# A two-layer encoder trunk on one core: four weight units by landed tile at the start, another SSD output chain, attention scores by row halves

## The chip, the core and the metric

The kernel runs on one core of a Trainium2 chip. A core has TensorE (PE, matrix products into PSUM), VectorE (DVE), ScalarE (ACT), GpSimd (POOL) and SyncE (SP, which here issues nearly all DMAs). PE's weight loads are listed apart as PEld. The metric is the device time of one execution in microseconds (us); the median of three runs before the change is 2410.8 us (2410.72 to 2411.09).

## The reference

512 tokens of 1024 features go through two layers of four steps. RMSNorm gains and residual sums are in every step:

```
h += 0.5 * swiglu(rmsnorm(h))                  # 1024 -> 2 x 2816 -> 1024
h += mixer(rmsnorm(h))                         # layer 0: SSD, layer 1: attention
h += 0.5 * swiglu(rmsnorm(h))
h += sigmoid(rmsnorm(h) @ Wg) * rmsnorm(p @ Wp)
```

The SSD mixer projects to z, x, B, C and dt, convolves, scans in both directions in chunks of 128 tokens, and ends with

```
y = rmsnorm(y * silu(z), norm_g)               # 2048 features
return y @ w_out
```

The attention has 16 heads of 64 features. The tokens form a grid of 8 x 64; queries go in four blocks of 16 columns (128 tokens), each against 32 columns (256 tokens):

```
q = rmsnorm(q, q_norm) * 64 ** -0.5 ;  k = rmsnorm(k, k_norm)
s = einsum(q_blk, k_blk) + bias                # 128 x 256 per head and block
o = einsum(softmax(s), v_blk)
```

## The kernel before

Activations lie with features on the 128 partitions and tokens along the free axis: `h[k]`, k = 0 to 7, are tiles of 128x512. Products are in float32 by three matmuls of a rounded type: a value is split into a high part (an ACT cast or activation, L183, L186) and the rest (a DVE subtraction, L184, L187); `gemm` (L172) multiplies high by high (L177), high weight by low activation (L178) and low weight by high activation (L179). Weights come in units of 128x1024: SP loads one into `wr` (L154, 4 buffers), ACT casts it to `wh` (L162), DVE subtracts to `wl` (L164); three split units are kept ready, so that the split made now is used some gemms later. One unit makes 24 matmuls of 128x512.

Norms are applied late: a gemm runs on gain times h, and its result is multiplied by the factor R. `SumSq` squares on ACT (L207) and adds on POOL (L211), the last addition on DVE. `rsqrt` (L213) spreads the sum by a matmul (L215) and takes Newton steps on 128x512; `begin` and `end` (L221, L231) are the short form: eight small matmuls (L225), Newton steps on 128x4, eight small matmuls (L235), an ACT copy (L238).

PSUM has five banks for gemms (`mm_bank`) and three for the rest (`px_bank`). Tiles come from pools by tag with a fixed number of buffers (`hs` 8, `t2` 7, `sc` 15, `sq` 4, `md` 24, `rt` 3); who takes a buffer waits for its last reader. A scheduler orders the instructions of each engine from the program; an engine then runs its own queue in order and waits where semaphores tell it to.

The places of the change:

- The start (L966 to L1000): the first two units are split by halves as their tiles land, and `first` runs their 48 matmuls by k, two banks in turn. The squares follow, and `ffn` (L273) takes the factor with `norm.factor()` after the second pair of units (f = 1).
- The SSD output: `out_half` (L698) multiplies y's first 1024 features beside the last head group's scan; `pairs_of` (L684) reads y back from `ydram` into `t` tiles (L690). Then eight gemms (d = 0 to 7) multiply the second half. For each d: DVE adds the first half from PSUM and SBUF (L739), POOL multiplies by the factor r2 (L740), DVE adds the residual (L744), and the next norm's split and square follow.
- The attention (L755 on): `project(j)` makes queries and values of head pair j in four pieces, and beside each piece the pairs already projected go on by one step of `attend`. `stack_keys` and `stack_queries` put the high and the low part of one head on the two partition halves, so that one score is two matmuls of 128 rows and 256 columns (L867). `turn` transposes a block's weights (L901), `weigh` multiplies by the values (L910), block by block.

Of the kernel before, what the change touches and what calls it, by code (L numbers as in the profile page):

```python
# [14 lines left out]
P = 128  # L15
# [32 lines left out]
def trunk(ctx, tc, A, out):  # L48
# [98 lines left out]
    todo, raws, ready = plan(), [], []  # L147
# [9 lines left out]
    def split_unit():  # L157
        load_unit()
        if raws:
            raw, n = raws.pop(0)  # L160
            hi = wp.tile([P, 1024], F32R, name=nm("wh"), tag="wh", bufs=3)
            s.copy(out=hi[:, :n], in_=raw[:, :n])  # L162
# [78 lines left out]
    class Norm:  # L241
# [15 lines left out]
        def count(self, k):  # L257
            self.ss.add(h[k], fast=k == KD - 1)
# [14 lines left out]
    def ffn(norm, nxt, between=lambda: None, first=None):  # L273
# [5 lines left out]
        def gate_up(f):  # L279
            pg, pu = mm_bank(), mm_bank()  # L280
# [4 lines left out]
            gemm(pg, unit(), norm.pairs)  # L285
            gemm(pu, unit(), norm.pairs)
# [109 lines left out]
    def ssd(norm, nxt):  # L396
# [288 lines left out]
        def pairs_of(ks, alloc):  # L685
            res = []
            for k in ks:
                if k < 14:
                    yt = t2()
# [3 lines left out]
                pr = alloc()  # L693
# [33 lines left out]
        for d in range(KD):  # L727
# [16 lines left out]
            v.tensor_add(out=h[d].rearrange("p (c r) -> p r c", c=64), in0=old.rearrange(rows, c=64),  # L744
# [4 lines left out]
    def attention(norm, nxt):  # L749
# [6 lines left out]
        def keys(js):  # L756
# [23 lines left out]
            for i in range(4):  # L780
# [4 lines left out]
                kn = hs()  # L785
                v.scalar_tensor_tensor(out=kn, in0=raw[i], scalar=gqk, in1=rb, op0=ALU.mult, op1=ALU.mult)
                kz.append(kn)

        def stack_keys(j):

            res = []
            for a in range(2):
                kk = md(F32R)
                src = kz[j][a * 64:(a + 1) * 64, :]
                own, other = slice(a * 64, (a + 1) * 64), slice((1 - a) * 64, (2 - a) * 64)
                s.copy(out=kk[own, 0, :], in_=src)
                s.copy(out=kk[other, 0, :], in_=src)
                for x in (own, other):
                    v.tensor_sub(out=kk[x, 1, :], in0=src, in1=kk[own, 0, :])
                res.append(kk)  # L800
            return res

        def stack_queries(qb):

            res = []
            for a in range(2):
                qq = bp.tile([P, T], F32R, name=nm("t2"), tag="t2", bufs=7)
                own, other = slice(a * 64, (a + 1) * 64), slice((1 - a) * 64, (2 - a) * 64)
                s.copy(out=qq[own], in_=qb[own])
                v.tensor_sub(out=qq[other], in0=qb[own], in1=qq[own])  # L810
                res.append(qq)
            return res
# [6 lines left out]
        def project(j):  # L819
# [8 lines left out]
            ks = stack_keys(j)  # L828
# [6 lines left out]
            qs = stack_queries(qb)  # L835
# [15 lines left out]
            made[j] = (bias, qs, ks, rq, vt)  # L851
# [4 lines left out]
        def attend(j):  # L856

            bias, qs, ks, rq, vt = made.pop(j)
            st, pT = {}, {}
            vk = None  # L860
            po = None

            def scores(b):
                pscore = px_bank()
                for a in range(2):
                    for x in range(2):
                        te.matmul(out=pscore[:, a * 256:(a + 1) * 256], lhsT=qs[a][:, b * P:(b + 1) * P],  # L867
                                  rhs=ks[a][:, x, KC0[b] * 8:KC0[b] * 8 + 256], start=x == 0, stop=x == 1)
                x = st[b] = sc()
                for a in range(2):  # L870
                    sl = slice(a * 256, (a + 1) * 256)
                    v.scalar_tensor_tensor(out=x[:, sl], in0=pscore[:, sl], scalar=rq[:, 2 * b + a:2 * b + a + 1],
# [13 lines left out]
            def values():  # L886
                vk_ = md()
                for half in range(2):
                    pv = px_bank()
                    for i in range(4):  # L890
                        b, u = 2 * half + i // 2, i % 2
                        k0 = KC0[b] * 8 + u * P
                        te.transpose(out=pv[:, i * P:(i + 1) * P], in_=vt[:, k0:k0 + P], identity=ident)  # L893
                    s.copy(out=vk_[:, half, :], in_=pv)
                return vk_.rearrange("p x (i d) -> p (x i) d", d=P)
# [9 lines left out]
            def weigh(b):  # L905
                y = pT.pop(b)
                for a in range(2):
                    for u in range(2):
                        i = 2 * a + u
                        te.matmul(out=po[a * 64:(a + 1) * 64, b * P:(b + 1) * P],  # L910
                                  lhsT=vk[:, 2 * b + u, a * 64:(a + 1) * 64], rhs=y[:, i * P:(i + 1) * P],
                                  start=u == 0, stop=u == 1)

            for t in range(7):
                if t < 4:
                    scores(t)
                if t == 0:
                    vk = values()
                if 2 <= t < 6:
                    turn(t - 2)  # L920
                if t == 3:
                    po = px_bank()
                if t >= 3:
                    weigh(t - 3)
                if t == 6:
                    op = opr[j] = md(F32R)
                    split(op, po, None)
                yield

# [24 lines left out]
        for d in range(KD):  # L954
# [3 lines left out]
            else:  # L958
# [11 lines left out]
    begun = [(next(todo),) + tuple(wp.tile([P, 1024], dt, name=nm(t), tag=t, bufs=b)  # L970
                                   for t, dt, b in (("wr", F32, 4), ("wh", F32R, 3), ("wl", F32R, 3)))
             for _ in range(2)]
    wcols = (slice(0, 512), slice(512, 1024))
    s.dma_start(out=cst[:, :C_GM], in_=A["cst"][:, :C_GM])
    s.activation(out=warm, in_=ones_d[:, 0:1], func=AF.Silu)
    for k in range(KD):
        sy.dma_start(out=h[k], in_=A["x"][:, k, :])
        if k in (0, 3):
            for src, raw, hi, lo in begun:
                sy.dma_start(out=raw[:, wcols[k // 3]], in_=src[:, wcols[k // 3]])  # L980
    load_unit()
    load_unit()
    sy.dma_start(out=cst[:, C_GM:], in_=A["cst"][:, C_GM:])
    sy.dma_start(out=msk, in_=A["msk"])
    for k in range(KD):
        n.prep(k, False)
        if k in (0, 3):
            for src, raw, hi, lo in begun:
                sl = wcols[k // 3]
                s.copy(out=hi[:, sl], in_=raw[:, sl])  # L990
                last_lo = v.tensor_sub(out=lo[:, sl], in0=raw[:, sl], in1=hi[:, sl])

    def first(pg, pu, pairs):
# [116 lines left out]
```

## Time and profile before

| | |
|---|---|
| median of three runs | 2410.8 us |
| profiled execution | 2410.27 us, span 2408.5 us |
| PE busy, granted clock | 2379.1 us (99%), 0.997 on the mean |
| DVE, ACT, POOL busy | 1441.3, 965.9, 461.7 us (60, 40, 19%) |
| attention stretch | about 1740 to 1960 us |
| SSD output, second half | about 889 to 957 us |

A busy share is a mean over the whole span. Idle time of an engine beside PE costs nothing unless PE waits for it; so the table says that PE is what the time is made of, and the few gaps in PE's own timeline are what other engines cost. A line number may be that of a helper: L187 is the split of any activation.

### The profile page before, as it was taken

The page shows a single profiled execution, that of the slowest core. Times are in us where ns is not written, and L with a number is a line of the kernel's source. Part 1 is how long each engine was busy: PE and PEld are TensorE (multiplying, and loading weights), DVE is VectorE, ACT ScalarE, POOL GpSimd, SP SyncE. Part 2 cuts the span into 40 slices and gives each one's busy share as a digit, 9 for nine tenths or more (in the row PEclk, how much of TensorE's full clock was granted, in tenths as well). Part 3 has the DMA queues.
Part 4 walks back from the last instruction along what each step waited for, and adds up shares of the span by engine and source line. Part 5 has one row for each costly group of instructions (what it writes and reads, how often), then busy time and mean ns, then how long its engine had stood idle before and what let it go on. Part 6 is the DMA issues. An engine that isn't in the chain of part 4 may idle for free.

```text
span 2408.5 us, 29115 instructions
## 1 busy us (share of the span) xinstructions
PE 2379.1 (99%) x11358; PEld 1953.1 (81%) x11358; DVE 1441.3 (60%) x1940; ACT 965.9 (40%) x1557; POOL 461.7 (19%) x387
## 2 busy tenths in 40 slices
PE   8999999999999998999999999999999999999999
PEld 6888888888888786888887888888777878888887
DVE  6544447877777746554447755444579965444456
ACT  4322224655555653332224433222337753222242
POOL 1110101344554544110003111000100011100120
PEclk9999999999999999999999999999999999999999
DMA  4333333544444542333333333333443323333332
GB/s 169 97 96 96 90 121 102 174 135 139 143 140 140 171 141 79 96 96 97 95 103 91 97 96 97 96 96 92 136 142 113 105 70 96 97 97 96 105 92 75
DMA packets 89418, 265.56 MB, mean 110 GB/s; under 512 B 10928, under 2 KB 11824, under 8 KB 89280
## 3 DMA queue, kind: packets, MB, share of 16 engines
q1 hardware_dynamic: 88992, 263.56, 35.5%
q8 instruction: 89, 1.46, 0.2%
q14 instruction: 49, 0.40, 0.1%
q10 hardware_dynamic: 288, 0.14, 0.0%
HBM read 253.40 MB, written 10.26 MB: 109 GB/s over the span
## 4 chain that ended last, share of the span: by engine, by line
PE 57%; DVE 4%; ACT 1%; POOL 1%; issue 0%; DMA 0%; SPq 0%; POOLq 0%; DVEq 0%
PE ps L178 18%; PE ps L177 18%; PE ps L179 18%; PE ps L910 1%; DVE wl L164 1%; PE ps L867 1%; PE ps L901 1%; DVE md L187 0%; DVE md L355 0%; POOL t L740 0%; DVE sc L198 0%; PE ps L773 0%; PE ps L893 0%; DVE sc L197 0%; DVE rt L199 0%
## 5 line engine op out<-in xcount | busy, mean ns | idle before, releaser
L177 PE MATMUL ps<-md,wh 128*128 128x512 f32 x3184 | 1252.2, 393 | 15.2 <-ACT md L186 9.2
L178 PE MATMUL ps<-md,wh 128*128 128x512 f32 x3184 | 1243.0, 390 | 3.3 <-DVE md L187 3.2
L179 PE MATMUL ps<-md,wl 128*128 128x512 f32 x3184 | 1241.8, 390 | 0.6 <-DVE wl L164 0.6
L162 ACT CAST wh<-wr 128x1024 fp32r<-128x1024 f32 (+1 forms) x403 | 416.5, 1034 | 1036.2 <-PE ps L178 655.5
L177 PEld LDWEIGHTS ps<-md,wh 128*128 128x128 f32 x3184 | 599.4, 188 | 147.2 <-ACT md L186 12.8
L178 PEld LDWEIGHTS ps<-md,wh 128*128 128x128 f32 x3184 | 599.5, 188 | 133.8 <-DVE md L187 7.1
L179 PEld LDWEIGHTS ps<-md,wl 128*128 128x128 f32 x3184 | 599.3, 188 | 125.2 <-DVE wl L164 1.1
L164 DVE TENSOR_TENSOR wl<-wr,wh 128x1024 fp32r<-128x1024 f32 (+1 forms) x403 | 579.6, 1439 | 148.4 <-ACT wh L162 119.4
L300 POOL TENSOR_TENSOR t<-t,sc 128x512 f32<-128x512 f32 x88 | 122.5, 1393 | 1017.8 <-ACT wh L162 741.9
L211 POOL TENSOR_TENSOR sq<-sq,sq 128x512 f32<-128x512 f32 x77 | 110.0, 1428 | 599.8 <-ACT sq L207 598.3
L299 DVE TENSOR_TENSOR t<-ps,rt 128x512 f32<-128x512 f32 x88 | 60.8, 691 | 262.0 <-PE ps L179 262.0
L310 DVE SCALAR_TENSOR_TENSOR hs<-ps,hs 128x512 f32<-128x512 f32 x96 | 66.3, 691 | 228.0 <-PE ps L179 228.0
L295 DVE TENSOR_TENSOR t<-ps,rt 128x512 f32<-128x512 f32 x88 | 60.8, 691 | 126.5 <-PE ps L179 126.4
L494 DVE SCALAR_TENSOR_TENSOR t<-ps,ccw,t 128x510 f32<-128x510 f32 (+1 forms) x180 | 134.0, 744 | 3.2 <-ACT t L490 0.3
L547 POOL TENSOR_TENSOR sc<-sc,sc 128x512 f32<-128x512 f32 x64 | 96.2, 1518 | 71.4 <-ACT sc L537 71.3
L183 ACT CAST md<-t 128x512 fp32r<-128x512 f32 x96 | 59.4, 623 | 124.0 <-POOL t L300 122.0
L535 ACT ACTIVATE sc<-hs,md 128x128 f32<-128x128 f32 x256 | 82.4, 397 | 1.7 <-DMA hs<-crow 1.7
L184 DVE TENSOR_TENSOR md<-t,md 128x512 fp32r<-128x512 f32 x96 | 66.8, 700 | 21.5 <-ACT md L183 21.1
L186 ACT ACTIVATE md<-hs,cst 128x512 fp32r<-128x512 f32 x64 | 45.9, 722 | 61.8 <-DVE hs L744 26.1
L187 DVE SCALAR_TENSOR_TENSOR md<-hs,cst,md 128x512 fp32r<-128x512 f32 x64 | 53.3, 843 | 14.6 <-ACT md L186 14.6
L497 ACT ACTIVATE t<-t 128x512 f32<-128x512 f32 x48 | 30.2, 630 | 79.1 <-DVE t L494 78.5
L562 POOL TENSOR_TENSOR md<-md,md 128x256 f32<-128x256 f32 x64 | 44.1, 723 | 80.6 <-ACT md L558 80.6
(155 smaller groups left out, 1362.7 us busy)
## 6 DMA issues: line engine op xcount, KB each, us to landing
wr<-in_w_gu_dram SPq DMA_DIRECT2D x174, 512.0 KB, 3.5
wr<-in_w_in_dram SPq DMA_DIRECT2D x65, 512.0 KB, 3.7
wr<-in_w_dn_dram SPq DMA_DIRECT2D x64, 448.0 KB, 3.3
wr<-in_w_dn_dram SPq DMA_DIRECT2D x32, 512.0 KB, 3.5
hs<-crow SPq DMA_DIRECT2D x64, 256.0 KB, 4.0
wr<-in_w_qkv_dram SPq DMA_DIRECT2D x24, 512.0 KB, 3.5
hs<-vrow SPq DMA_DIRECT2D x64, 128.0 KB, 3.5
wr<-in_w_out_dram SPq DMA_DIRECT2D x16, 512.0 KB, 4.1
```

The source lines that it names most:

```text
L162: s.copy(out=hi[:, :n], in_=raw[:, :n])
L164: v.tensor_sub(out=lo[:, :n], in0=raw[:, :n], in1=hi[:, :n])
L177: te.matmul(out=pt, lhsT=hi[:, sl], rhs=xp[:, 0, cols], start=first and k == 0, stop=False)
L178: te.matmul(out=pt, lhsT=hi[:, sl], rhs=xp[:, 1, cols], start=False, stop=False)
L179: te.matmul(out=pt, lhsT=lo[:, sl], rhs=xp[:, 0, cols], start=False, stop=last and k == n - 1)
L184: v.tensor_sub(out=dst[:, 1, :], in0=src, in1=dst[:, 0, :])
L211: (v if fast else g).tensor_add(out=self.acc, in0=self.acc, in1=q)
L300: g.tensor_mul(out=um, in0=um, in1=sg)
L310: v.scalar_tensor_tensor(out=h[d], in0=pt, scalar=0.5, in1=h[d], op0=ALU.mult, op1=ALU.add)
L494: v.scalar_tensor_tensor(out=a[:, lo:hi], in0=src[:, lo + o:hi + o], scalar=w(j), in1=a[:, lo:hi], op0=ALU.mult, op1=ALU.add)
L535: s.activation(out=e[:, cs(c)], in_=cb[:, cs(c)], func=AF.Relu, scale=-1.0, bias=cum[:, dr, c, hd:hd + 1])
L547: g.tensor_mul(out=es[j], in0=es[j], in1=cbm[j % 2])
```

## The change

Start: four units (gate and up of f = 0 and 1) are loaded and split by halves, in one list of 16 tiles with the eight of x; `first` goes through the list and runs, at each landed tile, all matmuls that it allows, on four banks. The statistics take the short form: `begin` after the 96 matmuls, `end` after the gate gemm of f = 2. All additions of squares are on DVE.

```diff
-            if first and f == 0:
-                first(pg, pu, norm.pairs)
+            if first and f < 2:
                 held.append((f, pg, pu))
+                if f == 1:
+                    first([p for x in held for p in x[1:]], norm.pairs)
+                    norm.begin()
                 return
             gemm(pg, unit(), norm.pairs)
+            if first and R[0] is None:
+                R[0] = norm.end()
+                while held:
+                    activate(*held.pop(0))
+                pu = mm_bank()
             gemm(pu, unit(), norm.pairs)
...
+    order = (0, (0, 0), (1, 0), 1, (2, 0), (3, 0), 2, 3, (0, 1), (1, 1), 4, 5, (2, 1), (3, 1), 6, 7)
...
+        for o in order:
+            if isinstance(o, int):
+                here = o + 1
+            else:
+                cut_[o[0]] += 1
+            for u in range(4):
+                while done_[u] < min(here, 4 * cut_[u]):
+                    k = done_[u]
+                    gemm(pts[u], begun[u][2:], pairs[k:k + 1], first=k == 0, last=k == KD - 1, off=k)
+                    done_[u] += 1
...
-                n.count(k)
+                n.count(k, True)
```

SSD output: y is read back into the second half of its own pair tile; POOL multiplies the first half by r2 and adds the residual for all d as soon as r2 is there.

```diff
+                pr = alloc()
                 if k < 14:
-                    yt = t2()
+                    yt = pr[:, 1, :].bitcast(F32)
                     sy.dma_start(out=yt, in_=ydram[k])
...
                 r2 = ss.end()
+                for k in range(KD):
+                    old = sc()
+                    sy.dma_start(out=old, in_=hd[k])
+                    g.tensor_mul(out=parts[k], in0=parts[k], in1=r2)
+                    g.tensor_add(out=parts[k], in0=parts[k], in1=old)
             pt = pts.pop(0)
-            old = sc()
-            sy.dma_start(out=old, in_=hd[d])
             u = t2()
-            v.tensor_add(out=u, in0=pt, in1=parts[d])
-            g.tensor_mul(out=u, in0=u, in1=r2)
+            v.tensor_mul(out=u, in0=pt, in1=r2)
...
-            v.tensor_add(out=h[d].rearrange("p (c r) -> p r c", c=64), in0=old.rearrange(rows, c=64),
+            v.tensor_add(out=h[d].rearrange("p (c r) -> p r c", c=64), in0=parts[d].rearrange(rows, c=64),
                          in1=u.rearrange(rows, c=64))
```

Attention: keys and queries are split once, in whole tiles; a score is three matmuls on the 64 rows of its head, the two heads in turns, two blocks in two banks. The division by the sum goes to POOL. The four blocks' products with the values come together at the end of a pair, the two heads (column halves) in turns.

```diff
+            def scores(bs):
+                pscore = [px_bank() for _ in range(2)]
+                for n, b in enumerate(bs):
+                    for i, (x, y) in enumerate(((0, 0), (0, 1), (1, 0))):
+                        for a in range(2):
+                            r_ = slice(a * 64, (a + 1) * 64)
+                            te.matmul(out=pscore[a][:, n * 256:(n + 1) * 256], lhsT=qs[x][r_, b * P:(b + 1) * P],
+                                      rhs=kj[r_, y, KC0[b] * 8:KC0[b] * 8 + 256], start=i == 0 and n == 0,
+                                      stop=i == 2 and n == 1)
...
-                    v.tensor_scalar(out=x[:, sl], in0=x[:, sl], scalar1=su[:, a:a + 1], scalar2=None, op0=ALU.mult)
+                    g.tensor_scalar(out=x[:, sl], in0=x[:, sl], scalar1=su[:, a:a + 1], scalar2=None, op0=ALU.mult)
...
+            def weigh(po):
+                for b in range(4):
+                    y = pT.pop(b)
                     for u in range(2):
+                        for a in range(2):
+                            i = 2 * a + u
...
+            for x in range(2):
+                scores((2 * x, 2 * x + 1))
+                values(x)
                 yield
+            for x in range(2):
+                turn(2 * x)
+                turn(2 * x + 1)
+                yield
+            po = px_bank()
+            weigh(po)
```

POOL at the end of the SSD output, before, from the first operation that needs r2 (`rt_7549`); `t_` are the sums of one d, `sq_` the squares of the next norm:

```order
L740 TENSOR_TENSOR t_7553<-t_7553,rt_7549 128x512 [waits DVE_49,Activation_49]
L740 TENSOR_TENSOR t_7596<-t_7596,rt_7549 128x512 [waits DVE_49]
L740 TENSOR_TENSOR t_7640<-t_7640,rt_7549 128x512 [waits DVE_49]
L211 TENSOR_TENSOR sq_7561<-sq_7561,sq_7604 128x512 [waits Activation_49]
L211 TENSOR_TENSOR sq_7561<-sq_7561,sq_7648 128x512 [waits Activation_49,Pool_49]
L740 TENSOR_TENSOR t_7684<-t_7684,rt_7549 128x512 [waits DMAHW5_49,DVE_49]
L211 TENSOR_TENSOR sq_7561<-sq_7561,sq_7692 128x512 [waits Activation_49,Pool_49]
```

The same place now; `md_` hold two of the first halves each, `sc_` the residuals (L747 is the product, L748 the sum):

```order
L747 TENSOR_TENSOR md_6953<-md_6953,rt_7553 128x512 [waits Activation_49]
L747 TENSOR_TENSOR md_6953<-md_6953,rt_7553 128x512
L748 TENSOR_TENSOR md_6953<-md_6953,sc_7555 128x512 [waits DMAHW7_49,Pool_49]
L748 TENSOR_TENSOR md_6953<-md_6953,sc_7559 128x512 [waits DMAHW0_49,Pool_49]
L747 TENSOR_TENSOR md_7096<-md_7096,rt_7553 128x512 x2
L748 TENSOR_TENSOR md_7096<-md_7096,sc_7563 128x512 [waits DMAHW1_49,Pool_49]
L748 TENSOR_TENSOR md_7096<-md_7096,sc_7567 128x512 [waits DMAHW3_49,Pool_49]
```

Sixteen such operations stand in a row, with no addition of squares between them; the six additions follow the sixteenth.

DVE at the same place, before, for one d after the first three (L164 is the subtraction of a weight unit that a later gemm uses):

```order
L739 TENSOR_TENSOR t_7684<-ps_7563,md_7086 128x512 [waits PE_49]
L164 TENSOR_TENSOR wl_7612<-wr_7514,wh_7610 128x1024 [waits DMAHW6_49,Activation_49]
L744 TENSOR_TENSOR hs_7687<-sc_7682,t_7684 128x8x64 [waits DMAHW1_49,Pool_49]
L187 SCALAR_TENSOR_TENSOR md_7689<-hs_7687,cst,md_7689 128x512 [waits Activation_49]
L739 TENSOR_TENSOR t_7728<-ps_7607,md_7187 128x512 [waits PE_49]
```

DVE now, around the weight subtractions of d = 6 and 7 (L751 multiplies from PSUM, L755 adds what POOL made):

```order
L755 TENSOR_TENSOR hs_7670<-md_7096,t_7668 128x8x64 [waits DVE_49,Pool_49]
L187 SCALAR_TENSOR_TENSOR md_7631<-hs_7629,cst,md_7631 128x512 [waits Activation_49]
L751 TENSOR_TENSOR t_7709<-ps_7596,rt_7553 128x512 [waits PE_49]
L164 TENSOR_TENSOR wl_7642<-wr_7467,wh_7640 128x1024 [waits DMAHW2_49,Activation_49]
L187 SCALAR_TENSOR_TENSOR md_7672<-hs_7670,cst,md_7672 128x512 [waits Activation_49]
L755 TENSOR_TENSOR hs_7711<-md_7096,t_7709 128x8x64 [waits DVE_49,Pool_49]
L187 SCALAR_TENSOR_TENSOR md_7713<-hs_7711,cst,md_7713 128x512 [waits Activation_49]
L751 TENSOR_TENSOR t_7750<-ps_7637,rt_7553 128x512 [waits PE_49]
L755 TENSOR_TENSOR hs_7752<-md_7197,t_7750 128x8x64 [waits DVE_49,Pool_49]
L164 TENSOR_TENSOR wl_7683<-wr_7518,wh_7681 128x1024 [waits DMAHW0_49,Activation_49]
```

Before, a weight subtraction stood ahead of the addition that waits for POOL; now two of these additions stand between one weight subtraction and the next.

PE in the attention, before, in the middle of one pair (L901 transposes, L867 scores, L893 transposes of the values, L910 values; L177 to L179 are the gemm beside them):

```order
L901 MATMUL ps_14029<-msk,sc_13934 128x128 [waits DVE_49]
L901 MATMUL ps_14029<-msk,sc_13934 128x128
L867 MATMUL ps_14040<-md_13782,t_13849 128x256 [waits PE_49]
L867 MATMUL ps_14040<-md_13782,t_13849 128x256
L867 MATMUL ps_14040<-md_13787,t_13852 128x256 x2
L177 MATMUL ps_14120<-md_13042,wh_13886 128x512
L893 MATMUL ps_14058<-msk,t_13965 128x128 [waits Activation_49]
L893 MATMUL ps_14058<-msk,t_13965 128x128 x3
L910 MATMUL ps_13991<-sc_14034,md_13820 64x128 x4
```

PE now, from one pair's last values to the next pair's first scores (L905 values, L855 scores, in two banks in turns):

```order
L905 MATMUL ps_14735<-sc_14675,md_14522 64x128 [waits Activation_49]
L905 MATMUL ps_14735<-sc_14675,md_14522 64x128 x3
L905 MATMUL ps_14735<-sc_14682,md_14522 64x128 x4
L905 MATMUL ps_14735<-sc_14703,md_14522 64x128 [waits Activation_49]
L905 MATMUL ps_14735<-sc_14703,md_14522 64x128 x3
L905 MATMUL ps_14735<-sc_14710,md_14522 64x128 [waits Activation_49]
L905 MATMUL ps_14735<-sc_14710,md_14522 64x128 x3
L855 MATMUL ps_14756<-md_13454,hs_14583 128x256 [waits PE_49]
L855 MATMUL ps_14757<-md_13454,hs_14583 128x256 [waits PE_49]
L855 MATMUL ps_14756<-md_13454,hs_14583 128x256
L855 MATMUL ps_14757<-md_13454,hs_14583 128x256
```

The values of a pair now stand together; twelve scores follow each other in alternating banks where four stood before.

## Rows read from the trace of the kernel before

**Rows 1.** The page's first part: busy us (share of the span) xinstructions.

```profile
PE 2379.1 (99%) x11358; PEld 1953.1 (81%) x11358; DVE 1441.3 (60%) x1940; ACT 965.9 (40%) x1557; POOL 461.7 (19%) x387
```

**Rows 2.** Timeline of PE, start: start us, us, what [idle before <-releaser].

```profile
11.53 0.39 PE L177 MATMUL ps<-md,wh 128*128 128x512 f32 x1
...
19.46 0.39 PE L179 MATMUL ps<-md,wl 128*128 128x512 f32 x1
23.90 1.29 PE L215 MATMUL ps<-sq,ones_d 128*128 128x512 f32 x2 [4.05 <-DVE sq L211]
...
48.27 0.39 PE L177 MATMUL ps<-md,wh 128*128 128x512 f32 x1
```

**Rows 3.** Timeline of POOL, start.

```profile
15.04 8.08 POOL L211 TENSOR_TENSOR sq<-sq,sq 128x512 f32<-128x512 f32 x6 [14.60 <-ACT sq L207]
```

**Rows 4.** Timeline of PE, head of the first output half.

```profile
830.37 0.96 PE L177 MATMUL ps<-md,wh 128*128 128x512 f32 x3 [0.51 <-ACT md L186]
```

**Rows 5.** Timeline of ACT, same place.

```profile
829.60 2.05 ACT L186 ACTIVATE md<-t,cst 128x512 fp32r<-128x512 f32 x3 [2.46 <-DMA t<-ydram]
```

**Rows 6.** Timeline of SP (its DMA issues), same place.

```profile
824.74 2.90 SPq L690 DMA_DIRECT2D t<-ydram  x6
```

**Rows 7.** Timeline of PE, end of the SSD output.

```profile
900.00 0.94 PE L225 MATMUL ps<-ones_d,sq 128*128 128x1 f32 x8
900.80 0.49 PE L177 MATMUL ps<-md,wh 128*128 128x512 f32 x1
...
942.22 0.49 PE L177 MATMUL ps<-md,wh 128*128 128x512 f32 x1 [3.47 <-ACT md L186]
...
948.24 0.79 PE L177 MATMUL ps<-md,wh 128*128 128x512 f32 x1 [4.01 <-ACT md L186]
...
957.00 1.02 PE L215 MATMUL ps<-sq,ones_d 128*128 128x512 f32 x2
```

**Rows 8.** Windows, attention: stretch and length, busy us by engine, clock, DMA.

```profile
1840.00:1940.00 100.00, 99.94 (x650) 79.18 (x649) 89.83 (x264) 70.63 (x163) 0.00 (x0) 1.00 0.31 98
```

**Rows 9.** Timeline of POOL, end of the SSD output.

```profile
908.15 4.97 POOL L740 TENSOR_TENSOR t<-t,rt 128x512 f32<-128x512 f32 x3 [14.78 <-ACT rt L238]
...
925.81 2.27 POOL L740 TENSOR_TENSOR t<-t,rt 128x512 f32<-128x512 f32 x1
```

**Rows 10.** Timeline of DVE, end of the SSD output.

```profile
909.89 5.23 DVE L744 TENSOR_TENSOR hs<-sc,t 128x512 f32<-128x512 f32 x3 [1.18 <-POOL t L740]
...
925.39 1.54 DVE L164 TENSOR_TENSOR wl<-wr,wh 128x1024 fp32r<-128x1024 f32 x1
...
948.22 0.75 DVE L187 SCALAR_TENSOR_TENSOR md<-hs,cst,md 128x512 fp32r<-128x512 f32 x1 [0.79 <-ACT md L186]
```

**Rows 11.** Timeline of PE: the scan's products in column halves, then attention.

```profile
711.98 1.97 PE L629 MATMUL ps<-sc,md 128*64 128x128 f32 x32
713.87 0.50 PE L177 MATMUL ps<-md,wh 128*128 128x512 f32 x1
...
1865.50 0.66 PE L910 MATMUL ps<-sc,md 128*64 128x128 f32 x8
1866.10 0.50 PE L177 MATMUL ps<-md,wh 128*128 128x512 f32 x1
...
1866.66 0.63 PE L867 MATMUL ps<-md,t 128*128 128x256 f32 x4
1867.13 0.40 PE L179 MATMUL ps<-md,wl 128*128 128x512 f32 x1
```

**Rows 12.** Groups by line and shape: busy us, mean ns | idle before.

```profile
L872 DVE SCALAR_TENSOR_TENSOR sc<-ps,sm,md 128x256 f32<-128x256 f32 x64 | 29.4, 476 | 8.4 <-PE ps L867 8.2
L879 ACT ACTIVATE sc<-sc,sm 128x256 f32<-128x256 f32 x64 | 32.0, 502 | 10.3 <-DVE sm L876 8.3 <-ACT sc L879 0.8 <-DVE sm L199 0.6
L884 DVE TENSOR_SCALAR sc<-sc,sm 128x256 f32<-128x256 f32 x64 | 20.0, 347 | 0.2
L562 POOL TENSOR_TENSOR md<-md,md 128x256 f32<-128x256 f32 x64 | 44.1, 723 | 80.6 <-ACT md L558 80.6
```

More of the change, by code (lines that the diff above doesn't have):

```diff
@@ L145, in plan @@
                     yield A["w_ao"][d]
-    todo, raws, ready = plan(), [], []
+    todo, raws, ready, splits = plan(), [], [], []
     def load_unit():
@@ L784, in keys @@
                     sy.dma_start(out=rb[r_], in_=rkd[2 * i + a:2 * i + a + 1, :].to_broadcast([64, T]))
-                kn = hs()
-                v.scalar_tensor_tensor(out=kn, in0=raw[i], scalar=gqk, in1=rb, op0=ALU.mult, op1=ALU.mult)
+                v.scalar_tensor_tensor(out=rb, in0=raw[i], scalar=gqk, in1=rb, op0=ALU.mult, op1=ALU.mult)
+                kn = md(F32R)
+                split(kn, rb, None)
                 kz.append(kn)
[L789 to L812, printed above, removed]
         made = {}
@@ L827, in project @@
             half_gemm(pt, w, 0)
-            ks = stack_keys(j)
             yield
@@ L834, in project @@
             s.activation(out=qq, in_=qb, func=AF.Square)
-            qs = stack_queries(qb)
+            qs = [bp.tile([P, T], F32R, name=nm("hs"), tag="hs", bufs=8) for _ in range(2)]
+            s.copy(out=qs[0], in_=qb)
+            v.tensor_sub(out=qs[1], in0=qb, in1=qs[0])
             yield
@@ L856, in attend, with soften @@
         def attend(j):
-            bias, qs, ks, rq, vt = made.pop(j)
+            bias, qs, kj, rq, vt = made.pop(j)
             st, pT = {}, {}
[L860 to L868, printed above, removed]
+            def scores(bs):
[7 more added lines that the diff above has]
+                                      stop=i == 2 and n == 1)
+                for n, b in enumerate(bs):
+                    soften(b, [p[:, n * 256:(n + 1) * 256] for p in pscore])
+            def soften(b, pscore):
                 x = st[b] = sc()
@@ L975, in trunk, with half, bring, cut @@
     s.activation(out=warm, in_=ones_d[:, 0:1], func=AF.Silu)
[L976 to L982, printed above, removed]
+    def half(x):
+        return slice(512 * x, 512 * x + 512)
+    def bring(u, x):
+        sy.dma_start(out=begun[u][1][:, half(x)], in_=begun[u][0][:, half(x)])
+    def cut(u, x):
+        src, raw, hi, lo = begun[u]
+        cast = s.copy(out=hi[:, half(x)], in_=raw[:, half(x)])
+        v.tensor_sub(out=lo[:, half(x)], in0=raw[:, half(x)], in1=hi[:, half(x)])
+        return cast
@@ L983, in trunk @@
+    order = (0, (0, 0), (1, 0), 1, (2, 0), (3, 0), 2, 3, (0, 1), (1, 1), 4, 5, (2, 1), (3, 1), 6, 7)
+    for o in order:
+        if isinstance(o, int):
+            sy.dma_start(out=h[o], in_=A["x"][:, o, :])
+        else:
+            bring(*o)
+    for _ in range(3):
+        load_unit()
     sy.dma_start(out=cst[:, C_GM:], in_=A["cst"][:, C_GM:])
     sy.dma_start(out=msk, in_=A["msk"])
[L985 to L991, printed above, removed]
@@ L993, in first @@
-    def first(pg, pu, pairs):
-        for k in range(KD):
-            for pt, (src, raw, hi, lo) in zip((pg, pu), begun):
-                gemm(pt, (hi, lo), pairs[k:k + 1], first=k == 0, last=k == KD - 1, off=k)
-        with tc.issue_after(n.last_cast.ins):
+    for o in order:
+        if isinstance(o, int):
+            n.prep(o, False)
+        else:
+            last_cut = cut(*o)
+    def first(pts, pairs):
+        done_ = [0] * 4
+        here, cut_ = 0, [0] * 4
+        for o in order:
+            if isinstance(o, int):
+                here = o + 1
+            else:
+                cut_[o[0]] += 1
[4 more added lines that the diff above has]
+                    done_[u] += 1
+        while len(ready) < 3:
+            split_unit()
+        with tc.issue_after(splits[-1].ins):
```

67 lines of the change are left out of this document (25 added, 42 removed).

## The prediction

> **What bounds the kernel now.** I read the page's first part first: TensorE (PE) is busy 99% of the span [rows 1]. So no other engine's total matters; the change can gain only where PE stands still or slows, or where PE work itself gets less. I then went through PE's timeline for every gap over 0.3 us in the stretches that the diff touches, and read beside each gap what POOL, VectorE (DVE) and ScalarE (ACT) do there. Three places lose time. At the start, PE has done its first 48 matmuls at 19.46 and then idles 4.05 us until the sum of squares is there [rows 2]; the six additions on POOL are what it waits for [rows 3]. At the head of the first half of the SSD output projection PE waits 0.51 us for an activation [rows 4] and soon again, and ACT has waited 2.46 us for data read back from DRAM [rows 5], whose reads were issued only at 824.74 [rows 6]. At the end of the SSD output PE idles 3.47 and 4.01 us before it has its last inputs [rows 7]. The attention stretch is the opposite: PE is busy 99.94 of 100 us there and DVE 89.83 [rows 8], so there only PE's own count of work and a newly late input can move the end.
>
> The profiled execution took 2410.27 us, 1.8 more than its span and 0.5 less than the median of 2410.8. I work in differences to its trace and add them to the median.
>
> **Start: -3.0 us.** A 128x512 matmul starts every 0.2266 us (35 steps from 11.53 to 19.46 [rows 2]). Instead of 48 matmuls on two banks, 96 on four now come before the statistics are wanted. If the tiles land as before and no pair is late, the 96th starts at 11.53 + 83 x 0.2266 = 30.3 and is done at 30.6. The statistics then go by the short form: eight small matmuls, 0.80 us like those of 900.00 [rows 7]; a gate unit of 24 x 0.2266 = 5.44; eight more, about 0.9. Now the up unit of f=2 wants a bank, which is free when f=0's product has been read: a copy (0.68 each in the ACT row [rows 5]), a weight subtraction queued ahead of that product and the product itself stand between, of which I let 1.8 us show. Then 5.44 again. Sum: 30.6 + 0.8 + 5.4 + 0.9 + 1.8 + 5.4 = 44.9, with 0.3 for the slower first matmul after each switch 45.2. That is 144 matmuls done; before, the 145th started at 48.27 [rows 2]. Gain 3.0; between 1 (if the 16 landings and 32 splits run behind PE, or the sum of squares is not ready by 30.6) and 4 (no bank wait). The seven additions of the statistics are DVE's now and have all of matmuls 48 to 96 as cover.
>
> **First output half: -1.2 us.** The values read back go straight into the second half of the pair tiles, so the reads no longer wait for t tiles: in SyncE's order they stand some 4 us earlier, behind the same vrow reads. The 0.51 and two like it go [rows 4]; I take 1.2. What is late next is the pace of ACT and DVE themselves: three activations took 2.05 us [rows 5], 0.68 each, as much as the three matmuls that one of them feeds (3 x 0.2266), with no slack; so between -2 and +1.
>
> **SSD output tail: +5 us.** Before, each of eight d took a DVE addition from PSUM, a POOL product, a DVE addition, then activation and split. Now POOL makes `parts * r2 + old` for all eight d at once after r2: 16 operations instead of 8, and DVE only multiplies from PSUM and adds. The trace shows what these cost beside each other. POOL's three products and DVE's three additions from SBUF, in the same microseconds, fill 908.15 to 915.12 [rows 9, 10]: six operations in 6.97 us, 1.16 each, in turns. A POOL product that meets a weight subtraction takes 2.27, and the subtraction 1.54 [rows 9, 10]. So DVE operations with two SBUF inputs and POOL operations use one lane here, and their times add. That lane now holds, from 908.15 on: 16 POOL operations x 1.2 = 19.2, eight additions x 1.1 = 9.0 (the 6.97 us less three POOL operations, by three), eight splits of 0.7 = 5.6 (0.75 alone [rows 10]), five weight subtractions at the same 1.2, an estimate, 6.0, and three of the six POOL additions of squares that get in before the end, 3.7: 43.5 us, to 951.6. The last pair was split at 948.97 before (948.22 + 0.75 [rows 10]); so even with no gap in the lane nothing is won. There are gaps: DVE's queue puts the weight subtractions of d=6, d=7 and the next gate unit behind additions that wait for POOL's product and sum of a later d (the order shown under the change), so PE runs out of weights that were ready before: worked through by turns, those of d=6 are ready at 926.3 against 923.5 wanted (900.80 [rows 7] plus four gemms of 5.44 and 0.9 for the small matmuls), d=7's at 937, the gate's at 943.5, and the last split at 955.3, 6.3 later than before. One matmul group and the whole up unit follow it, as now, when the next matmul came at 957.00 [rows 7]; I take +5, since the 27 matmuls from 948.24 to 957.00 took 8.8 us where 27 x 0.2266 is 6.1, and with other gaps ahead of them some of those 2.7 may come back. The bounds: -8, if POOL's operations ran beside DVE's at 1.2 us each (16 x 1.2 = 19.2, ready at 927, and the loss of 11 us around 942.22 and 948.24 would shrink to some 3), and +9, if the first POOL operations also wait for the reads of `old`.
>
> **Attention: -0.2 us.** Scores: 128 matmuls of 256 columns over the full array, four in 0.47 us (1866.66 to 1867.13 [rows 11]), 128 x 0.1175 = 15.0 us, become 192 that use one half of the rows each, in turns, into two banks. No such pair is in this trace. Two ends: both halves run together, 0.0588 each, 11.3 us; or one after the other, 0.1175, 22.6 us. What limits such a pair is read from the nearest rows: eight matmuls of a single column with a new 128-column weight block each take 0.80 us, 0.10 each [rows 7], which can only be the loading of weights; with 64-column blocks 32 matmuls take 1.89 us, 0.059 each (711.98 to 713.87 [rows 11]). Each of the 192 loads a 128-column block, so I take 0.10: 19.2 us, +4.2.
>
> The Trainium skill ("TensorE: Matmul & The Clock Gate", Step-by-step) says that the loading time goes by columns and not by rows, which speaks against this part; by it alone the term is the one taken, and a plain count of rows would give the 0.0588. The trace agrees in that half the columns took 0.059 instead of 0.10; for half the rows it shows nothing.
>
> Values: before 32 groups of eight, 0.60 each (1865.50 to 1866.10) and the matmul after them 0.10 longer [rows 11], 22.4 us; now eight groups of 32 in column halves in turns, the form of 711.98: 8 x 1.97 and the switch, 16.2. Gain 6.2. Transposes go in 16 groups instead of 32, 0.1 less each time: -1.5. Switching into and out of row halves 16 times: +1.5, the same 0.1 each as an estimate. The normalisation by 1/sum moves from DVE (64 x 347 ns) to POOL, where a 128x256 operation takes 723 ns [rows 12]. The chain for blocks 2 and 3 is, for one block, two reads of PSUM (2 x 476 ns), a maximum over 512 (0.7, an estimate), two exponentials (2 x 502), small operations (0.6) and two POOL operations (2 x 723): 4.7 us [rows 12]; the second block ends about 2 later. Against that 6.7 stand 7.4 us of PE work between the scores and their transposes: 24 matmuls, 5.4, and three groups of small ones, about 2; I take 0.3 us of waiting for each of the eight pairs: +2.4, bounds 0 and +8. DVE loses the stacked keys and queries, off the path; at the entry of the stretch it frees perhaps 0.6. Sum: 4.2 - 6.2 - 1.5 + 1.5 + 2.4 - 0.6 = -0.2.
>
> **Sum.** -3.0 - 1.2 + 5.0 - 0.2 = +0.6, so 2411.4 us: no change that can be told (0.2% is 4.8 us, about what a measurement can tell). Own range 2405 to 2417.
>
> **Rivals.**
> *Row halves overlap.* Weight loads and streams of the two halves run side by side: 0.0588 instead of 0.10, 7.9 us less: 2403.5. For it: the two halves have nothing in common in SBUF, and write different banks. Against: the column halves at 711.98 go in turns too and come no faster than 0.059 for 128 columns, which is the pace of one stream. The Trainium skill ("TensorEngine Tiling (Array Packing)", Key Properties) says that different tiles can load and multiply in parallel; no run here shows it. Chance 0.26.
> *The SSD tail is shortened as written.* POOL's 16 operations run in their own 1.2 us: -8 instead of +5: 2398.4. Against it are the six operations in 6.97 us. Chance 0.12.
> *POOL and DVE share the lane in attention too.* Slower: POOL had nothing there [rows 8]; now 64 operations x 0.72 = 46 us meet DVE's weight subtractions, which grow from 1.2 to 1.54 as at 925.39 [rows 10] and hold POOL up as long as at 925.81 [rows 9], and the chain to the transposes grows past the 7.4 us. From the point where each pair waits over 0.9 us it decides; at 1.2 us a pair it is +9.6 instead of +2.4: 2418.6. For it: DVE 89.83 busy before; against it: DVE loses 20.0 us for these 64 alone [rows 12]. Chance 0.19.
> The forecast keeps 0.43, of which 0.08 lie on the faster side of 0.2% and 0.06 on the slower.
>
> Faster: 0.26 + 0.12 less 0.06 of the first rival that stays within 0.2%, plus 0.08 = 0.40. Slower: 0.19 + 0.06 = 0.25. Same: 0.35. The range reaches nearly to the second rival and past the third: 2399 to 2421.
>
> **What would show it.** Start: 96 matmuls without a gap, and the 145th at about 45.2. First half: no activation that waits for ydram. Tail: POOL operations of about 2 us where DVE has two SBUF inputs, matmuls waiting for weight subtractions at about 924 and 932, and the FFN's up unit ending 5 us later relative to the SSD's last scan work. Attention: twelve score matmuls in 1.2 us (0.7 would be the first rival), 32 value matmuls in 2 us, and waits of 0.3 us for POOL before the second pair of transposes. I am wrong if the tail gets shorter, or if twelve scores take 0.8 us or less.

## The result and the profile after

The changed kernel takes 2420.83 us (2418.68 to 2421.97, five runs) where the kernel before takes 2410.72: ratio 1.0043, 95% interval 1.0028 to 1.0058. It is 10 us slower, and no change was forecast.

PE's timeline can be cut at the same instructions in both kernels: the norm and statistics matmuls (L215, L225, L235) and the scan's products in column halves (L629). The starts of these give the length of each stretch in us:

| stretch | before | after | difference |
|---|---|---|---|
| start to the SSD's norm | 380.11 | 377.30 | -2.8 |
| to the scan's 14th group (825.71 before) | 445.60 | 445.85 | +0.2 |
| first output half, to the last group | 59.88 | 59.21 | -0.7 |
| to the SSD's statistics | 14.41 | 16.87 | +2.5 |
| SSD output to the FFN's norm | 57.00 | 60.81 | +3.8 |
| first gate gemm of layer 0's last step | 6.43 | 8.04 | +1.6 |
| attention, norm to norm | 264.17 | 270.18 | +6.0 |
| all others together | | | -0.1 |

**Start.** PE's timeline after, to be read beside [rows 2]:

```profile
30.57 0.95 PE L225 MATMUL ps<-ones_d,sq 128*128 128x1 f32 x8
...
36.96 1.05 PE L235 MATMUL ps<-msk,sm 128*128 128x128 f32 x8
39.89 0.50 PE L177 MATMUL ps<-md,wh 128*128 128x512 f32 x1 [1.88 <-DVE t L304]
...
45.46 0.39 PE L177 MATMUL ps<-md,wh 128*128 128x512 f32 x1
```

The 4.05 us of idle time are gone, the wait for the bank is 1.88, and the 145th matmul starts at 45.46 instead of 48.27.

**First output half.** The reads of y are issued from 817.84 on, and the waits for an activation are gone from PE's timeline. What is left are waits for DVE's splits, of which the longest is:

```profile
832.39 0.50 PE L178 MATMUL ps<-md,wh 128*128 128x512 f32 x1 [1.29 <-DVE md L187]
```

**Ahead of the second output half.** The last pair of activations comes from the last head group. PE after:

```profile
890.30 0.50 PE L177 MATMUL ps<-md,wh 128*128 128x512 f32 x1 [0.98 <-ACT md L186]
891.59 0.50 PE L178 MATMUL ps<-md,wh 128*128 128x512 f32 x1 [0.79 <-DVE md L187]
891.92 0.40 PE L179 MATMUL ps<-md,wl 128*128 128x512 f32 x1
892.16 0.59 PE L177 MATMUL ps<-md,wh 128*128 128x512 f32 x1
892.55 0.63 PE L178 MATMUL ps<-md,wh 128*128 128x512 f32 x1
892.98 0.63 PE L179 MATMUL ps<-md,wl 128*128 128x512 f32 x1
```

DVE, then POOL, at the same place:

```profile
884.40 0.75 DVE L642 SCALAR_TENSOR_TENSOR sc<-md,cst,ps 128x512 f32<-128x512 f32 x1
885.07 1.22 DVE L164 TENSOR_TENSOR wl<-wr,wh 128x1024 fp32r<-128x1024 f32 x1
```

```profile
885.23 3.01 POOL L668 TENSOR_TENSOR sc<-sc,hs 128x384 f32<-128x384 f32 x2 [9.26 <-DVE sc L642]
```

The weight subtraction now stands behind the head's product (L642) and starts 0.16 us ahead of POOL's two additions, which take 3.01 us. PE then waits twice (once before, 0.79 us), and matmuls follow each other at 0.43 us, the lower of its two clock levels (1.2 GHz), where they came every 0.2266 before the waits. The granted clock, last but two in a window's row, is 0.66 there:

```profile
891.50:896.50 5.00, 4.92 (x14) 3.88 (x15) 1.26 (x2) 1.05 (x1) 0.00 (x0) 0.66 0.55 200
```

**SSD output's end.** PE after, beside [rows 7]:

```profile
924.68 0.50 PE L179 MATMUL ps<-md,wl 128*128 128x512 f32 x1 [1.20 <-DVE wl L164]
930.76 0.50 PE L177 MATMUL ps<-md,wh 128*128 128x512 f32 x1 [0.77 <-ACT wh L162]
934.26 0.80 PE L179 MATMUL ps<-md,wl 128*128 128x512 f32 x1 [2.77 <-DVE wl L164]
...
950.35 0.80 PE L177 MATMUL ps<-md,wh 128*128 128x512 f32 x1 [1.81 <-ACT md L186]
```

POOL and DVE there, beside [rows 9, 10]:

```profile
919.77 3.77 POOL L747 TENSOR_TENSOR md<-md,rt 128x512 f32<-128x512 f32 x2
923.50 3.98 POOL L748 TENSOR_TENSOR md<-md,sc 128x512 f32<-128x512 f32 x2
```

```profile
922.91 1.71 DVE L164 TENSOR_TENSOR wl<-wr,wh 128x1024 fp32r<-128x1024 f32 x1
...
931.96 2.24 DVE L164 TENSOR_TENSOR wl<-wr,wh 128x1024 fp32r<-128x1024 f32 x1
...
950.50 0.74 DVE L187 SCALAR_TENSOR_TENSOR md<-hs,cst,md 128x512 fp32r<-128x512 f32 x1
```

POOL's sixteen operations take 1.3 to 2.1 us each, 28 us in all (907.37 to 935.33), and PE waits for weights (wl) in the middle of gemms, which it did not in this stretch before. The last split ends at 951.24, though the stretch began 0.8 earlier.

**Attention.** The window of [rows 8], then the groups of the POOL division and of the transposes behind it:

```profile
1840.00:1940.00 100.00, 92.66 (x665) 72.45 (x663) 72.89 (x207) 57.66 (x144) 43.49 (x46) 1.00 0.29 96
```

```profile
L877 POOL TENSOR_SCALAR sc<-sc,sm 128x256 f32<-128x256 f32 x64 | 60.3, 957 | 166.9 <-DVE sm L874 125.8 <-PE ps L855 32.2 <-PE ps L895 3.0
...
L895 PE MATMUL ps<-msk,sc 128*128 128x128 f32 x128 | 22.5, 284 | 8.8 <-POOL sc L877 8.3 <-DVE sm L869 0.4
```

One pair on POOL, and on PE:

```profile
1854.31 3.62 POOL L877 TENSOR_SCALAR sc<-sc,sm 128x256 f32<-128x256 f32 x4 [7.60 <-DVE sm L874]
1858.61 3.62 POOL L877 TENSOR_SCALAR sc<-sc,sm 128x256 f32<-128x256 f32 x4 [0.67 <-DVE sm L193]
```

```profile
1849.03 0.97 PE L855 MATMUL ps<-md,hs 64*128 64x256 f32 x12
1849.93 0.50 PE L177 MATMUL ps<-md,wh 128*128 128x512 f32 x1
...
1862.28 0.44 PE L895 MATMUL ps<-msk,sc 128*128 128x128 f32 x2 [0.46 <-POOL sc L877]
1862.65 1.97 PE L905 MATMUL ps<-sc,md 128*64 128x128 f32 x32
```

PE fell from 99.94 to 92.66 busy of 100 us. Twelve scores take 0.90 us (1849.03 to 1849.93), quicker than before (four took 0.47 [rows 11]); but POOL's eight divisions of a pair fill 1854.31 to 1862.23 but for 0.67 us between the fours, and the transposes come in pieces as each division ends.

### The profile page after: what moved, and what is told of

It reads as the page before. It is cut to its first block, busy times and chain, and to the rows that moved or that the text cites. A ratio compares the mean times of both kernels' runs of the same rounds, so it can differ in the third digit from the quotient of the medians.

```text
span 2419.0 us, 29330 instructions
## 1 busy us (share of the span) xinstructions
PE 2382.1 (98%) x11436; PEld 1954.1 (81%) x11436; DVE 1416.7 (59%) x1852; ACT 946.3 (39%) x1528; POOL 531.1 (22%) x453
## 4 chain that ended last, share of the span: by engine, by line
PE 84%; DVE 6%; issue 5%; POOL 4%; ACT 1%; DMA 0%; SPq 0%; POOLq 0%; DVEq 0%; ACTq 0%
PE ps L178 26%; PE ps L177 26%; PE ps L179 26%; POOL sc L877 1%; DVE wl L164 1%; PE ps L638 1%; POOL sc L556 1%; PE ps L617 1%; PE ps L659 1%; DVE md L187 1%; PE ps L905 1%; PE ps L577 1%; PE ps L563 1%; POOL sc L668 0%; DVE md L364 0%
## 5 line engine op out<-in xcount | busy, mean ns | idle before, releaser
L177 PE MATMUL ps<-md,wh 128*128 128x512 f32 (+1 forms) x3152 | 1241.2, 394 | 6.7 <-ACT md L186 4.0
L178 PE MATMUL ps<-md,wh 128*128 128x512 f32 (+1 forms) x3152 | 1231.3, 391 | 5.2 <-DVE md L187 5.1
L179 PE MATMUL ps<-md,wl 128*128 128x512 f32 (+1 forms) x3152 | 1230.7, 391 | 4.6 <-DVE wl L164 4.6
L177 PEld LDWEIGHTS ps<-md,wh 128*128 128x128 f32 x3152 | 594.1, 188 | 133.8 <-ACT md L186 5.8
L179 PEld LDWEIGHTS ps<-md,wl 128*128 128x128 f32 x3152 | 594.0, 188 | 130.0 <-DVE wl L164 6.2
L164 DVE TENSOR_TENSOR wl<-wr,wh 128x1024 fp32r<-128x1024 f32 (+1 forms) x401 | 578.7, 1443 | 163.4 <-ACT wh L162 129.4
L183 ACT CAST md<-t 128x512 fp32r<-128x512 f32 x96 | 59.4, 623 | 122.5 <-POOL t L309 120.6
L877 POOL TENSOR_SCALAR sc<-sc,sm 128x256 f32<-128x256 f32 x64 | 60.3, 957 | 166.9 <-DVE sm L874 125.8
```

The costliest lines, as they stand in the source:

```text
L177: te.matmul(out=pt, lhsT=hi[:, sl], rhs=xp[:, 0, cols], start=first and k == 0, stop=False)
L178: te.matmul(out=pt, lhsT=hi[:, sl], rhs=xp[:, 1, cols], start=False, stop=False)
L179: te.matmul(out=pt, lhsT=lo[:, sl], rhs=xp[:, 0, cols], start=False, stop=last and k == n - 1)
L877: g.tensor_scalar(out=x[:, sl], in0=x[:, sl], scalar1=su[:, a:a + 1], scalar2=None, op0=ALU.mult)
```

## The experiments

Times of one kernel spread by some us from run to run, and the spread goes with the clock that TensorE was granted: twenty runs of the kernel before go from 2407.29 us at a mean granted clock of 0.998 to 2417.39 at 0.994. So beside the medians I compare the stretches of the table.

Each kernel has one trace, and one trace is one sample. How far it can be trusted is seen where kernels share the code of a stretch:

| stretch | kernels with the same code there | us |
|---|---|---|
| first output half, old reads | 4 | 59.9 |
| first output half, new reads | 6 | 59.2 to 61.1 |
| to the SSD's statistics, old reads | 4 | 14.4 |
| to the SSD's statistics, new reads | 6 | 15.3 to 16.9 |
| SSD output's end, old chain | 3 | 56.5 to 57.7 |
| SSD output's end, new chain | 6 | 59.6 to 60.8 |
| attention, division on POOL | 3 | 269.4 to 270.2 |
| attention, both row halves, division on DVE | 4 | 257.0 to 257.3 |

**The division back on DVE.**

```diff
-                    g.tensor_scalar(out=x[:, sl], in0=x[:, sl], scalar1=su[:, a:a + 1], scalar2=None, op0=ALU.mult)
+                    v.tensor_scalar(out=x[:, sl], in0=x[:, sl], scalar1=su[:, a:a + 1], scalar2=None, op0=ALU.mult)
```

> The changed kernel with the division by the softmax sum back on DVE, all else as changed. Theory (POOL): the attention's loss is the wait for POOL's 64 divisions of 0.92 us (DVE took 0.35); by PE's own count of work the stretch is 6.8 us shorter than before (scores 14.4 instead of 15.0, values 16.2 instead of 22.4), and it came out 6.0 longer, so up to 12.8 us go: 2408 to 2412, and the stretch between the two large norm matmuls 253 to 258 us instead of 270.2. Rival (grouping): the wait comes from the transposes standing in groups of eight behind two blocks' scores, whichever engine divides: 2419 to 2421, the same stretch 268 or more.

Measured: 2408.48 us, ratio to before 0.9991 (0.998 to 1.0002). The attention stretch is 257.07 us: 13.1 less than with POOL and 7.1 less than before. The window:

```profile
1840.00:1940.00 100.00, 99.48 (x748) 79.97 (x747) 84.50 (x269) 60.28 (x156) 0.00 (x0) 1.00 0.33 103
```

The transposes stand in the same groups, and PE is busy 99.48; so the loss was POOL's division, not the grouping. The group of these transposes, to be read beside the L895 above, shows where the 13.1 us were:

```profile
L895 PE MATMUL ps<-msk,sc 128*128 128x128 f32 x128 | 18.7, 275 | 0.3 <-DVE sc L877 0.2
```

Idle time ahead of them is 0.3 us instead of 8.8, and they are busy for 18.7 instead of 22.5: 12.3 of the 13.1.

**The SSD output's end as before.**

```diff
-                for k in range(KD):
-                    old = sc()
-                    sy.dma_start(out=old, in_=hd[k])
-                    g.tensor_mul(out=parts[k], in0=parts[k], in1=r2)
-                    g.tensor_add(out=parts[k], in0=parts[k], in1=old)
...
-            v.tensor_mul(out=u, in0=pt, in1=r2)
+            v.tensor_add(out=u, in0=pt, in1=parts[d])
+            g.tensor_mul(out=u, in0=u, in1=r2)
...
```

> The changed kernel with the SSD output's end as before (DVE adds from PSUM, POOL multiplies by r2 once per d, DVE adds the residual); reads, start and attention as changed. Theory (one lane): the stretch from the short statistics to the FFN's norm matmul goes back from 60.8 to about 57.0 us, 2417.0. Rival (the clock): the 3.8 us are low-clock time that falls where it falls; the stretch stays within 1 us of 60.8.

Measured: the stretch went from 60.81 to 57.70 us; 3.1 of the 3.8 us are the new chain's. The median, 2421.08 (2416.19 to 2424.73), is above the 2417 that I expected and too scattered to show it.

**y read back into its own tiles as before.**

```diff
-                pr = alloc()
                 if k < 14:
-                    yt = pr[:, 1, :].bitcast(F32)
+                    yt = t2()
...
+                pr = alloc()
                 split(pr, yt, col(C_SN + k))
```

> The changed kernel with y read back into t tiles as before. Theory (order): the 2.5 us lost ahead of the second output half come from the weight subtraction that now stands behind the last head's product on DVE and meets POOL's two additions there; with the old reads it stands ahead of it again, so this place gives back 2.5 and the first half loses its 0.7: 2419.0. Rival (the end's longer queue causes it): the place stays as it is and only the 0.7 are lost, 2421.5.

Measured: 2419.91 us; the stretch ahead of the statistics went back from 16.87 to 14.40, the first half from 59.21 to 59.86. POOL's two additions there, with the weight subtraction ahead of L642 again:

```profile
886.38 2.09 POOL L668 TENSOR_TENSOR sc<-sc,hs 128x384 f32<-128x384 f32 x2 [9.32 <-DVE sc L642]
```

2.09 instead of 3.01. So the reads cost time by an order that they changed 60 us later. How much, the other traces tell. In the kernel with the division on DVE, which has the new reads, PE has the same two waits (0.99 and 0.79 us), and then the full clock:

```profile
892.70:897.70 5.00, 4.89 (x21) 4.05 (x22) 1.28 (x2) 1.05 (x1) 0.00 (x0) 1.00 0.54 197
```

There the stretch takes 15.30 us, not 16.87: the order costs 0.9, and the lower clock behind the waits another 1.6, in four of the six traces with the new reads. The gain of 0.7 in the first half is not shown: of those six traces one has 59.2, one 59.4, three 59.8 to 59.9 as with the old reads, and one 61.1.

**One head's scores after the other's** (division on DVE).

```diff
-                    for i, (x, y) in enumerate(((0, 0), (0, 1), (1, 0))):
-                        for a in range(2):
+                    for a in range(2):
+                        for i, (x, y) in enumerate(((0, 0), (0, 1), (1, 0))):
```

> As the kernel with the division on DVE, but the three scores of one head after the other's three instead of in turns. Theory (row halves overlap only where neighbours use different halves): twelve scores take about 1.3 us instead of 0.90, so 16 groups cost 6 us more than with the division on DVE alone. Rival (a half-height matmul is cheaper by itself, or its weights are loaded ahead in any order): 0.9 as before, no difference.

Measured: attention 256.96 us, 2408.04 by the median. Twelve scores take 0.91, not the 1.3 of my theory:

```profile
1848.47 0.98 PE L855 MATMUL ps<-md,hs 64*128 64x256 f32 x12
1849.38 0.49 PE L178 MATMUL ps<-md,wh 128*128 128x512 f32 x1
```

The turns are not needed. That left two reasons, which the next two kernels separate.

**All scores on the lower 64 rows, and all on 128 rows** (division on DVE; the first computes the second head from the first's rows, the second sums over both heads).

```diff
-                            r_ = slice(a * 64, (a + 1) * 64)
+                            r_ = slice(0, 64)
```

> As the kernel with the division on DVE, but all scores use the lower 64 rows of keys and queries (the second head of a pair is computed from the first's rows). Theory (overlap of the two halves): with one half alone nothing overlaps, a score takes 0.1175 and twelve 1.41 us, so the attention stretch grows from 257.0 to about 265. Rival (a matmul of 64 rows is cheaper by itself): twelve take 0.90 as before, stretch 257.

```diff
-                            r_ = slice(a * 64, (a + 1) * 64)
+                            r_ = slice(0, 128)
```

> As the kernel with the division on DVE, but all scores use all 128 rows (each score then sums over both heads). It is the control for the run with 64 rows: twelve at the pace of the kernel before, 0.1175, are 1.41 us and the stretch about 265. If twelve take 0.90 here too, neither the half height nor an overlap is what makes them quick, but that twelve stand together.

PE with the lower rows alone, then with all rows:

```profile
1845.88 1.70 PE L855 MATMUL ps<-md,hs 64*128 64x256 f32 x12
1847.51 0.50 PE L178 MATMUL ps<-md,wh 128*128 128x512 f32 x1
```

```profile
1847.87 1.70 PE L855 MATMUL ps<-md,hs 128*128 128x256 f32 x12
1849.40 0.39 PE L178 MATMUL ps<-md,wh 128*128 128x512 f32 x1
...
1851.01 1.61 PE L855 MATMUL ps<-md,hs 128*128 128x256 f32 x12
1852.46 0.60 PE L886 MATMUL ps<-msk,t 128*128 128x128 f32 x4
```

Twelve take 1.63 us with one half (0.136 each), 1.45 to 1.53 with all rows (0.12 to 0.13), 0.91 with both halves (0.076). So half a height is not cheaper by itself; the two halves overlap, though not in full.

The stretches are 264.21 and 260.01 us. That the first is near its forecast of 265 is luck: twelve took 1.63, not 1.41, yet the stretch grew by 7.1 and not by 16 x 0.72 = 11.5. The second missed its 265; it grew by 2.9 and not by 16 x 0.6 = 9.6. In both, the neighbours of a group are quicker. The matmul behind a pair's first group takes 0.57 us with both halves, 0.34 with the lower rows alone and 0.24 with all rows, and part of the 0.57 is a wait of the transposes behind it. The weight loads (PEld) of the changed kernel there:

```profile
1850.51 0.42 PEld L886 LDWEIGHTS ps<-msk,t 128*128 128x128 f32 x4 [0.39 <-DVE md L184]
```

With longer groups this wait is gone. What going into and out of row halves costs is then about 0.1 us each: 0.32 instead of 0.23 for the matmul ahead of a pair's second group, 0.34 instead of 0.24 for the one behind its first.

**The parts that gained, and the SSD output without POOL.** First: start and attention as changed, division on DVE, reads and end of the SSD output as before.

> The start and the attention as changed with the division on DVE; reads and end of the SSD output as before. By the stages of the runs so far: start -2.8, attention -7.1, the rest as before: 2400 to 2401 where the kernel before is 2410. Rival (the gains are given back by the clock at other places): 2405 or more.

Measured: 2400.8 us (2398.79 to 2405.03), ratio 0.9967 (0.9956 to 0.9978). The stretches: 376.14 to the SSD's norm, 56.53 for the end, 257.03 for attention. Then, on top of it:

```diff
...
-            g.tensor_mul(out=u, in0=u, in1=r2)
+            v.tensor_mul(out=u, in0=u, in1=r2)
...
-            nxt(d)
+            nxt(d, fast=True)
```

> As the last, and at the end of the SSD output the product by r2 and the additions of squares go to DVE as well, so that POOL has nothing there. Theory (one lane, and a loop over POOL and DVE in it): before, one d takes 6.1 us of products, additions and squares in turns, more than the gemm's 5.44; on DVE alone it is 0.7 + 1.2 + 0.7 + 1.1 + 0.7 + 0.7 = 5.1, less than the gemm, so only the last one shows: the stretch falls from 57.0 to 46 to 49 us, 2391 to 2394. Rival (DVE becomes the bound, because all the work is on it): 57 us or more, 2400 or more.

Measured: 2395.26 us (2394.0 to 2396.59), ratio 0.9937 (0.9925 to 0.995): faster than both kernels. The end takes 50.60 us instead of 57.00, less gain than expected. DVE, one d of the steady part:

```profile
936.72 0.68 DVE L748 TENSOR_TENSOR t<-ps,md 128x512 f32<-128x512 f32 x1
937.32 1.22 DVE L164 TENSOR_TENSOR wl<-wr,wh 128x1024 fp32r<-128x1024 f32 x1
938.45 0.68 DVE L749 TENSOR_TENSOR t<-t,rt 128x512 f32<-128x512 f32 x1
939.17 1.08 DVE L753 TENSOR_TENSOR hs<-sc,t 128x512 f32<-128x512 f32 x1
941.04 0.75 DVE L187 SCALAR_TENSOR_TENSOR md<-hs,cst,md 128x512 fp32r<-128x512 f32 x1 [0.79 <-ACT md L186]
```

No weight subtraction is stretched there any more (all take 1.22 or 1.23); what I left out is the 0.79 us in which DVE waits for ACT, so that one d takes 5.66 (931.06 to 936.72), still over the gemm's 5.44, and one wait of 3.30 us remains ahead of the FFN.

## Why the prediction was wrong

By stretches the forecast missed by 6.2 us in attention, by 2.5 at the head of the second output half, which it did not count, and by 1.6 at a place where the two kernels do not differ; the other misses nearly cancel.

*Start:* right. Forecast: 96th matmul at 30.3, wait 1.8, 145th at 45.2; measured 30.34, 1.88, 45.46.

*First output half:* the gain was 0.7 in this trace instead of 1.2, and none in most traces with the same reads: the waits for activations went, and 1.29 us for a split on DVE came. The edit's cost was not in the forecast at all. I looked at the eight early reads and left out what the new order does at the second half's head: +2.5, shown by putting the reads back, of which 0.9 is the order's and 1.6 the clock's. I took the last pair's chain there as given; it passes through POOL, and one weight subtraction in its way is enough.

*SSD output's end:* right in its steps. Weights of d=6 forecast for 926.3, of d=7 for 937, last split 955.3 (each less the 0.8 by which the stretch began earlier); measured 924.62, 934.20, 951.24, so the lane was up to 3 us less full than worked out. Forecast +5, measured +3.8, undone -3.1. The Trainium skill ("SBUF — State Buffer", Terms) says that VectorE and GpSimd share a port pair that one of them holds for a whole instruction. The trace agrees: POOL's sixteen operations took 1.3 to 2.1 us each beside DVE, and with no POOL there DVE's 1.54 and 2.24 fell to 1.22.

*Attention:* this step failed (-0.2 forecast, +6.0 measured), in two terms with opposite signs. "I take 0.3 us of waiting for each of the eight pairs: +2.4" was the term that decided; the division on POOL cost 13.1 us, 1.6 a pair, over the upper end of +8 that I gave. One division took 0.92 us, not the 723 ns of an addition of the same shape [rows 12]; the view of the line gives 917/923 ns as least and median, so it is slow by itself and hardly held up by DVE. So the third rival's mechanism was not it, and that its 2418.6 us lie near the result is luck. And I followed one block's chain, with two divisions in it, while POOL does the four of two blocks in one row of 3.62 us. That row then holds up more than its own transposes. ACT in the pair shown:

```profile
1856.67 0.59 ACT L897 COPY sc<-ps 128x512 f32<-128x512 f32 x1 [1.32 <-PE ps L895]
1857.15 0.51 ACT L872 ACTIVATE sc<-sc,sm 128x256 f32<-128x256 f32 x1
```

The third block's exponentials (L872) stand behind the copy of the first block's transposed weights (L897), which waits for the transposes and so for POOL; the second row of divisions starts at 1858.61, after them. With the division on DVE these exponentials stand ahead of the copies. Of the 13.1 us, 12.3 lie at the transposes: 8.5 of idle time, and 3.8 of longer busy time, as they come in pieces; the last 0.8 is open. The other term: "I take 0.10" for a score; it measured 0.076, so scores gained 0.6 instead of losing 4.2. That closes the sum: without the wait the forecast was -2.6, and with the division on DVE the stretch is 7.1 shorter, 4.5 more. The values came as forecast (32 in 1.90 us, 1862.65 to 1864.55). The first rival was right that the halves overlap; its 0.0588 was too low. The Trainium skill ("TensorEngine Tiling (Array Packing)", Key Properties) says that different tiles work in parallel; the runs agree (0.91 us against 1.63). The Trainium skill ("TensorE: Matmul & The Clock Gate", Step-by-step) also says that the loading time goes by columns and not by rows; the runs agree, as 64 rows alone were no quicker than 128. My error was to take a bound on one half's loads as a bound on two.

*The clock:* 1.6 us lie where the two kernels have the same instructions. Ahead of the first gate gemm of layer 0's last step, PE waits 0.62 and 0.54 us (0.55 in the kernel before); before, 24 matmuls follow at the full clock, after, this:

```profile
1326.46 0.50 PE L177 MATMUL ps<-md,wh 128*128 128x512 f32 x1 [0.62 <-ACT md L186]
1327.50 0.50 PE L178 MATMUL ps<-md,wh 128*128 128x512 f32 x1 [0.54 <-DVE md L187]
...
1329.65 0.63 PE L178 MATMUL ps<-md,wh 128*128 128x512 f32 x1
1330.08 0.63 PE L179 MATMUL ps<-md,wl 128*128 128x512 f32 x1
```

```profile
1328.20:1336.20 8.00, 8.00 (x33) 6.70 (x33) 3.01 (x13) 0.93 (x1) 0.00 (x0) 0.79 0.36 122
```

The stretch takes 6.4, 8.0 or 9.7 us in the ten traces, over kernels that do not differ there. I have no run that tells what decides it, nor whether the change makes the loss likelier.

## What to carry to other kernels

Before moving work to an idle engine, price the operation itself on that engine, and then all its instances that fall into one burst, as a queue; the slack of one chain is not the slack of the queue, and what other engines have queued behind its results waits too. Where two engines alternate on one lane, moving an operation from the chain to the other engine made nothing shorter here; taking one engine out of the stretch did. Cut traces at common instructions, so that a change of several parts shows each part's sign: here gains at the start and in the attention's matmuls hid behind three losses. Then look at the same stretch in every trace that shares its code before believing a difference of less than 2 us.

## What the runs showed that I had not expected

A 128x256 multiplication by a per-partition factor takes 923 ns on POOL and 349 on DVE, and on POOL more than an addition of two tensors (723). Two row halves of 64, in runs of three or in turns, bring a 256-column matmul from 0.12 to 0.13 us (all rows) or 0.136 (one half alone) down to 0.076. And the same two waits of about half a microsecond leave PE at its full clock in one execution and cost 1.6 or 3.2 us at the lower level in another.
